# Gate vectors of a two-block transformer kernel: from one SBUF partition on ScalarE's queue to a DRAM copy on GpSimd's queue

## The chip, the cores and the metric

The kernel runs on one core of a Trainium2 chip. The metric is device time in microseconds, the median of several executions. All arithmetic is float32; large products are made of three passes, each on operands that were split into a high and a low part.

## The reference

A sequence of 256 tokens `x` (1024 features) and a context of 256 tokens `ctx` pass two blocks. The first has two layers. Each layer draws six vectors per stream from `c` (for the context from `c_ctx`): shift, scale and gate before and in each sublayer. The gates `g1`, `g2` are what this change touches.

```
m_lat = (silu(c) @ ada_w[i] + ada_b[i]);  m_ctx = silu(c_ctx) @ ada_w[i] + ada_b[i]
sh1, sc1, g1, sh2, sc2, g2 = split(m_lat, 6);  csh1, ..., cg2 = split(m_ctx, 6)
h, hc = rms(x) * (1 + sc1) + sh1, rms(y) * (1 + csc1) + csh1
o, oc = mixer(h, hc)              # layer 0: Fourier + window attention; layer 1: neighbourhood attention
x = x + g1 * o
x = x + g2 * swiglu(rms(x) * (1 + sc2) + sh2)
if not last: the same for the context y with cg1, cg2
```

The second block (retention, convolution, dilated attention, four swiglu) has no gates; it takes gains `norm_w_2` from DRAM.

## The kernel before

Tokens lie on partitions in two tiles of 128; each stream's activations transposed (`hT`, high and low part) are the stationary or moving side of the products. `Weights` (L205) streams the weights as blocks of 1 MB through three raw buffers on the SP queue: `load` (L242) issues the copy, `split` (L279) casts a block on ScalarE to its high part (`whi`) and subtracts on VectorE to its low part (`wlo`), by halves, into one of a few places. Every engine runs its instructions in the order of emission. That order is steered by `Pace` (L66), an account of when each engine would come to what has been emitted; it is an estimate of the program's own and moves nothing on the chip by itself. Its `note` (L127) charges a DMA issue with 1050 ns on GpSimd and 50 ns on another engine, and moves its one DMA clock `self.dma` on by the size of what is copied.

All instructions pass one helper (L60), so the profile's rows have that line; tile names tell them apart: `wraw` raw weight block, `acc` and `mm` PSUM, `hn` the normed tile, `ny` the inverse root on GpSimd, `jk` a sum of squares on ScalarE, `gate` a gate vector on all partitions, `rows` the six vectors as they come out.

The vectors are made in groups of 2048 outputs: group 0 is (sh1, sc1), group 1 (g1, sh2), group 2 (sc2, g2). `ada_unit` (L2093) multiplies one of eight blocks of inputs and adds the result into `rows`, a tile whose row 32 j (for x) and 32 j + 1 (for the context) hold outputs 512 j to 512 j + 511; at the first of the eight, the bias is loaded into it by GpSimd's queue. A gate vector thus lies in two single partitions, 512 numbers in each. `mods` (L2113) turns shift and scale into columns. `gate` (L2139) copies a gate to all 128 partitions, two DMAs on ScalarE's queue:

```
for h in range(2):
    r = 32 * (2 * x + h) + e
    nc.scalar.dma_start(out=t[:, h * 512:h * 512 + 512], in_=rows[r:r + 1, :]
                        .rearrange("p (a n) -> p a n", a=1).to_broadcast([1, 128, 512]))
```

The target is tile `gpost` (x) or `gpre` (context) of the pool `nb_p`, which hold one tile each and also serve layer 0's attention (its transposed probabilities `pt` and its mask), layer 1's `pt`, and the second block's gains (`gain`, L379, a GpSimd DMA from DRAM by `bcast_row`: one row of 1024 numbers for every partition). `gated` (L2150) multiplies the accumulator by the gate on VectorE and adds it to x.

`gate` is called at four places: in `Even.emit` before the output product (L1919, both streams), in the first feed-forward pair at its block 5 (L2182, both streams), in `Odd.emit` at its second quarter (L2073, x only) and in the second feed-forward at its block 5 (L2184, x only): six gates, twelve DMAs. In `Even.emit` the units of groups 1 and 2 are `fill`, work between the attention's steps: eight of group 1, then eight of group 2, so that sixteen additions to `rows` follow each other on VectorE. The output product of `Even` goes by `begin` and `tail` (two blocks for both token tiles, then the last two for tile 0 and for tile 1), first for x and then for the context. Layer 1's units are spread over the feed-forward pair (groups 0 and 1) and over `Odd` (group 2).

Of the kernel before, what the change touches and what calls it, by code (L numbers as in the profile page):

```python
# [7 lines left out]
F32 = mybir.dt.float32  # L8
# [4 lines left out]
PSUM = bass.MemoryType.PSUM  # L13

D = 1024
KD = 8
# [8 lines left out]
HOLD = 1200                # no split where a stage is due within this time ...  # L25
HOLD_AHEAD = 1             # ... unless fewer blocks than this are split ahead

# columns of the packed small inputs
# [9 lines left out]
# columns of the packed constants  # L38
# [11 lines left out]
class Engine:  # L50
    """Passes an engine's instructions on and keeps the pace's account of them."""
# [14 lines left out]
class Pace:  # L66
    """An estimate of when each engine comes to the instructions emitted so far, from the waits that
    the data needs and the price of each instruction. It only steers the order of emission."""

    LAG = {"pe": 190, "act": 40, "dve": 190, "pool": 190}       # from an engine's end to another's start  # L70
    OWN = {"pe": 0, "act": 190, "dve": 125, "pool": 125}        # ... to its own next instruction
# [12 lines left out]
    def entry(self, ap):  # L84
        """Times of the last write, of its engine, and of the last use, by element of the tile."""
        t = ap.tensor
        if t.name not in self.tiles:
            n = int(np.prod(t.shape[1:]))
            free = 0.0
            hist = self.tags.setdefault(t.tag, [])  # L90
            bufs = t.bufs or t.tag_meta.bufs
            if len(hist) >= bufs:
                free = max(x.max() for x in self.tiles[hist[-bufs]][:2])
            hist.append(t.name)
            self.tiles[t.name] = [np.full(n, free), np.full(n, free), ""]
        return self.tiles[t.name]
# [14 lines left out]
    def ready(self, *aps):  # L111
        """When the data of these is there for another engine."""
        return max(float(self.view(x, self.entry(x)[0]).max()) + self.LAG.get(self.entry(x)[2], 0) for x in aps)

    def free(self, tag, bufs, n):
        """When the next n tiles of this tag are free."""
# [3 lines left out]
    def loaded(self, tile):  # L120
        """A block of weights goes into this tile."""
# [45 lines left out]
    def clock(self, start, end):  # L167
        """The tensor engine runs at half its clock after a window in which it was mostly idle."""
# [36 lines left out]
class Weights:  # L205
    """Streams weight blocks: DRAM -> raw -> (high part, low part), ahead of their use.

    Blocks are split, by halves, where the pace has them landed and the engines that split them idle,
    so that no engine waits on a transfer with other work behind it."""

    def __init__(self, K):
# [4 lines left out]
        self.at = -1             # the last block asked for  # L216
        self.part = None         # the block of which one half is split
# [4 lines left out]
        self.slots = []          # free slots, the longest free first  # L222
# [11 lines left out]
    def close_slot(self, name):  # L234
        """No block goes into this slot any more."""
# [43 lines left out]
    def split(self, u):  # L279
        """The next half of block u."""  # L280
# [45 lines left out]
class Kernel:  # L326
# [3 lines left out]
    def open(self, ex):  # L330
# [13 lines left out]
        self.mm_n, self.held = 0, []         # tiles "mm" taken so far; those that put-off stages read: [number, task]  # L344
# [12 lines left out]
    def open_ext(self, n):  # L357
        """Room for one more weight block ahead; "3" is the place of the context's h^T."""
# [25 lines left out]
    def post(self, gain, bias=None):  # L384
        """x += rms(acc (+ bias)) * gain, in stages."""
# [31 lines left out]
    def block2(self, bin_):  # L417
        """bin_: the boundary before the first sublayer, its A of both tiles done."""
# [10 lines left out]
    def table(self, func):  # L429
        """Have the scalar engine fetch this function's table ahead of its use."""  # L430
# [13 lines left out]
    def rsqrt(self, ss, n, scale, eps, pool, tag="n", bufs=None):  # L444
        """1/sqrt(ss * scale + eps)."""
# [6 lines left out]
    def square(self, ss, src, b):  # L452
        """ss[:, b] = sum of the squares / D of src, half b of [tok, D]."""
# [4 lines left out]
    def rstd(self, ss):  # L458
        """1/sqrt(ss[:, 0] + ss[:, 1] + eps)."""
# [9 lines left out]
    def split_psum(self, hi, lo, ps, act=True):  # L469
        """hi + lo = ps exactly, each with the bits one fast pass carries."""  # L470
# [4 lines left out]
    def bcast_row(self, row, n):  # L475
        """DMA source: a DRAM row of n elements for every partition."""
        return bass.AP(row.tensor, row.offset, [[0, 128], [1, n]])

# [7 lines left out]
    def mm32(self, out, lhsT, rhs, start, stop, share=1, **k):  # L486
        """A float32 product; share: how many run side by side."""
# [7 lines left out]
    def mm_nat(self, key, hT, t, out, parity=False):  # L495
        """out[tok, 256] = h[tok tile t, or the tokens of parity t] @ w block (K = 1024)."""
# [7 lines left out]
    def mm_trans(self, key, hT, out, need=1):  # L504
        """out[feat, j, tok] = (h @ w block)^T for its two 128-feature tiles."""
# [26 lines left out]
    def room(self, tag, n):  # L532
        """Run put-off tasks of this tag until fewer than n are left."""
# [6 lines left out]
    def defer(self, f, src, need=1, tag=None):  # L540
        """Run f (which takes `need` PSUM tiles) once the tensor engine has come to where src is there."""
# [7 lines left out]
    def stage(self, f, src, eng, tag=None, after=None):  # L549
        """Emit f, work of the engine eng, once that engine need not wait for src and `after` holds."""  # L550
# [4 lines left out]
    def run(self, task):  # L555
        """Run a put-off task now, if it hasn't run."""
# [10 lines left out]
    def poll(self, need=3):  # L567
        """Run what is due, as long as it takes no more than `need` PSUM tiles."""
# [10 lines left out]
    def soon(self):  # L579
        """Whether a stage is about to be due."""  # L580
        return any(x[4] and x[0] <= self.t + HOLD and (x[5] is None or x[5]()) for x in self.tasks)

    def tick(self):
        """Run the stages that are due."""
# [17 lines left out]
    def acct(self, shape=(128, 512)):  # L602
        """Two banks."""
# [3 lines left out]
    def new_hT(self, e=0):  # L607
        """The place of x's (of the context's) h^T: high and low parts."""
# [6 lines left out]
    def transposed(self, h, halves=None):  # L615
        """The transposes of h[tok, 1024] in PSUM, by halves."""
# [5 lines left out]
    def transpose_h(self, halves, hT, t, cols=None):  # L622
        """Transposes of tile t into h^T's high and low parts; cols: (scale, shift) columns."""
# [19 lines left out]
    def transpose_into(self, src, chunk, t):  # L643
        """src[tok, 256] of tile t, transposed, into a chunk's high and low parts."""
# [12 lines left out]
    def begin(self, keys, chunks):  # L657
        """The first two blocks where the boundary before still holds the accumulators: tile 0 first."""
# [9 lines left out]
    def tail(self, keys, chunks, bound, start=0, accs=None, mid=None, late=False):  # L668
        """The last blocks of acc[t] = sum over blocks of chunk^T @ w: token tile 0 ends first."""
# [22 lines left out]
    def head(self, keys, fn, bound):  # L692
        """The first blocks of a product take token tile 0 before tile 1 is ready."""
# [17 lines left out]
class Bound:  # L711
    """What lies between two sublayers: the residual update and the next sublayer's h^T."""
# [9 lines left out]
    def load(self, which=(True, True)):  # L722
        """Fetch the gains, if any, of the norms after and before a sublayer of the second block."""
# [7 lines left out]
    def tile(self, t):  # L731
        """Where tile t's h comes to stand."""
# [6 lines left out]
    def A(self, t, acc=None):  # L739
        """The update by tile t's acc and the norm, in stages."""  # L740
# [16 lines left out]
        # tile 1 after tile 0's transposes  # L757
# [24 lines left out]
    def put_off(self, t):  # L782
        """Have the transposes done when tile t's h is there."""
# [18 lines left out]
class Ffn:  # L802
    """swiglu: (silu(h wg) * (h wu)) wd."""
# [11 lines left out]
    def order(self):  # L815
        """(kind, index) in the order of use."""
# [84 lines left out]
class FfnPair:  # L901
    """swiglu of x and of the context, on one pass over the weights of its first product: what the
    context's half of the second product takes waits on chip."""
# [23 lines left out]
    def emit(self, bins, bouts):  # L927
        K, nc, W = self.K, self.K.nc, self.K.W
        name, n, cut = self.name, self.NP, self.CUT
        with K.tc.tile_pool(name=f"{name}_sg", bufs=2, reuse_waits="tile") as sg_p, \  # L930
# [4 lines left out]
            def finish(p, js, q, e):  # L935
                """silu(g) * u of the feature tiles js: x's split, the context's kept."""
# [10 lines left out]
            def head(units):  # L947
                """Units (block, g or u, x or the context) whose operands come one after the other."""
# [71 lines left out]
class Retention:  # L1020
# [4 lines left out]
    def order():  # L1025
        """(kind, head, part) in the order of use; of the first head, what can take a token tile at a time comes first."""
# [17 lines left out]
    def emit(self, bin_, bout):  # L1044
# [6 lines left out]
        # decay by distance: exp(lgf * max(n - m, 0) + lgb * max(m - n, 0)), column n - m + 128 of row m  # L1051
# [122 lines left out]
class Conv:  # L1174
    PADL = 15
    W = 288                  # columns of a padded row of tokens
# [12 lines left out]
    def emit(self, bin_, bout):  # L1189
# [19 lines left out]
        def shift(p):  # L1209
            """Rows (j, i): channel i of each group of 32, from token j - 15 on."""  # L1210
# [32 lines left out]
        def glu(p, s, qa, qb):  # L1243
            """(qa + bias) * sigmoid(qb + bias), features on the partitions, tokens s."""
# [12 lines left out]
        def build():  # L1257
            """The products' weights for the next part of the convolution."""
# [9 lines left out]
        def conv(kt, c0, n, nat):  # L1268
            """Depthwise: four taps and 32 channels a product, four of them side by side."""
# [24 lines left out]
        def stats(t, b):  # L1294
            """Layernorm over channels in the natural layout, then back."""
# [55 lines left out]
        bout.hT = oT             # token tile by token tile, what comes next takes its place  # L1351
# [23 lines left out]
class Attn:  # L1375
    """Softmax attention of two heads by 128 queries a step; scores, transposes and values lie apart."""
# [16 lines left out]
    def require(self, pred=lambda step: True):  # L1393
        """Go on until no step for which pred holds is open."""
# [61 lines left out]
    def turn(self, step, sm):  # L1456
# [4 lines left out]
        w = 4 // n               # heads to a PSUM tile  # L1461
# [137 lines left out]
class Even:  # L1599
    """Layer 0's mixer: Fourier mixing and attention, for x and for the context."""  # L1600
# [769 lines left out]
```

## Time and profile before

| | |
|---|---|
| time, median of 3 runs | 2721.39 us (2714.77, 2721.39, 2721.40) |
| profiled execution, first to last instruction | 2716.9 us; nothing is listed around it |
| mean granted TensorE clock | 0.985 |
| TensorE busy | 2599.4 us (96%) |
| VectorE, ScalarE, GpSimd busy | 1496.4, 1202.4, 108.5 us |
| DMA | 453.68 MB, 167 GB/s over the span |

The profiled execution's own time is its span. The share of busy time is a mean over stages; what one stage waits for is read in the timeline, where `[4.78 <-ACT whi L60]` says that the engine sat idle for 4.78 us before this instruction and what it then waited for. A "q" behind an engine (ACTq, SPq) is that engine's sequencer, which issues DMAs.

### The profile page before, as it was taken

What the parts mean: (1) busy time and instruction counts of PE and PEld (TensorE: products, weight loads), DVE (VectorE), ACT (ScalarE), POOL (GpSimd) and SP (SyncE); (2) the same over time, 40 slices, a digit from 0 to 9 for tenths busy, and PEclk for the clock granted to TensorE, in tenths of its full rate; (3) what the DMA queues carried; (4) which work ended last, traced back from release to release, by engine and by line L of the source; (5) the groups of instructions that cost most, each with busy time, mean ns of one, the idle gap of its engine ahead of it and who ended that gap; (6) DMA issues with size and microseconds to landing.
All of it is one profiled execution on the core that took longest, in us unless ns stands there. A gap on an engine that the chain in (4) does not pass through costs nothing.

```text
span 2716.9 us, 43849 instructions
## 1 busy us (share of the span) xinstructions
PE 2599.4 (96%) x18444; PEld 2308.7 (85%) x18444; DVE 1496.4 (55%) x2420; ACT 1202.4 (44%) x2050; POOL 108.5 (4%) x156
## 2 busy tenths in 40 slices
PE   6988997999989999999999979999999999999998
PEld 5646875788867999999999869989998999999997
DVE  4475332346647745765645555456555654765643
ACT  4454221235535544544544434445554544544532
POOL 1100000000311000000000000000000000000000
PEclk9998998999989999999999999999999999999999
DMA  7368257545464675564655736545443654564652
GB/s 259 123 215 153 102 185 125 189 155 184 119 129 137 202 176 181 181 199 142 206 182 168 226 89 212 192 140 175 136 132 118 210 186 155 181 202 140 205 186 82
DMA packets 321414, 453.68 MB, mean 167 GB/s; under 512 B 20689, under 2 KB 280913, under 8 KB 316097
## 3 DMA queue, kind: packets, MB, share of 16 engines
q1 hardware_dynamic: 315552, 434.63, 48.1%
q10 hardware_dynamic: 2592, 5.33, 3.7%
q0 software_dynamic: 3072, 10.91, 1.1%
q8 instruction: 145, 2.38, 0.4%
q14 instruction: 53, 0.43, 0.0%
HBM read 445.47 MB, written 2.23 MB: 165 GB/s over the span
## 4 chain that ended last, share of the span: by engine, by line
PE 83%; DVE 6%; DMA 6%; ACT 2%; issue 1%; ACTq 0%; POOL 0%; SPq 0%; DVEq 0%; POOLq 0%
PE mm L60 62%; PE acc L60 21%; DVE wlo L60 2%; DMA wraw<-ev_w_out 1%; DMA wraw<-ada_w 1%; DMA wraw<-ffn_w_up 1%; DVE sm L60 1%; DVE hTl L60 1%; ACT whi L60 1%; DMA u<-up 1%; DMA wraw<-ffn_w_down 1%; ACTq L60 0%; DMA taps<-u 0%; POOL ny L60 0%; DVE hn L60 0%
## 5 line engine op out<-in xcount | busy, mean ns | idle before, releaser
L60 DVE TENSOR_TENSOR wlo<-wraw,whi 128x1024 fp32r<-128x1024 f32 x592 | 701.3, 1225 | 454.4 <-ACT whi L60 453.5
L60 ACT CAST whi<-wraw 128x1024 fp32r<-128x1024 f32 x592 | 592.4, 1048 | 392.7 <-issue 155.7
L60 PE MATMUL mm<-hTh,whi 128*128 128x256 f32 (+1 forms) x1840 | 553.5, 301 | 17.0 <-ACT whi L60 15.2
L60 PE MATMUL mm<-hTh,wlo 128*128 128x256 f32 (+1 forms) x1840 | 552.0, 300 | 0.6 <-DVE wlo L60 0.5
L60 PE MATMUL mm<-hTl,whi 128*128 128x256 f32 (+1 forms) x1840 | 551.9, 300 | 0.3 <-DVE hTl L60 0.3
L60 PE MATMUL mm<-whi,hTh 128*128 128x256 f32 x1616 | 467.8, 290 | 4.1 <-ACT hTh L60 3.2
L60 PE MATMUL mm<-whi,hTl 128*128 128x256 f32 x1616 | 458.7, 284 | 5.5 <-DVE hTl L60 5.5
L60 PE MATMUL mm<-wlo,hTh 128*128 128x256 f32 x1616 | 457.9, 283 | 0.0
L60 PEld LDWEIGHTS mm<-hTh,whi 128*128 128x128 f32 x1840 | 352.7, 192 | 32.0 <-ACT whi L60 16.0
L60 PEld LDWEIGHTS mm<-hTl,whi 128*128 128x128 f32 x1840 | 351.7, 191 | 13.5 <-DVE hTl L60 0.5
L60 PEld LDWEIGHTS mm<-hTh,wlo 128*128 128x128 f32 x1840 | 351.6, 191 | 13.0 <-DVE wlo L60 1.7
L60 PEld LDWEIGHTS mm<-whi,hTh 128*128 128x128 f32 x1616 | 310.4, 192 | 22.7 <-issue 9.7
L60 PEld LDWEIGHTS mm<-whi,hTl 128*128 128x128 f32 x1616 | 310.4, 192 | 7.6 <-DVE hTl L60 7.6
L60 PEld LDWEIGHTS mm<-wlo,hTh 128*128 128x128 f32 x1616 | 310.9, 192 | 0.6
L60 PE MATMUL acc<-whi,ckh 128*128 128x512 f32 x664 | 264.7, 399 | 0.0
L60 PE MATMUL acc<-whi,ckl 128*128 128x512 f32 x664 | 262.6, 395 | 0.6 <-DVE ckl L60 0.6
L60 PE MATMUL acc<-wlo,ckh 128*128 128x512 f32 x664 | 262.6, 395 | 0.4 <-DVE wlo L60 0.4
L60 PE MATMUL mm<-hTh 128*128 128x256 f32 x656 | 188.3, 287 | 0.5 <-ACT hTh L60 0.5
L60 PE MATMUL mm<-hTh,hTl 128*128 128x256 f32 x656 | 186.7, 285 | 0.4 <-DVE hTl L60 0.4
L60 PE MATMUL mm<-hTl,hTh 128*128 128x256 f32 x656 | 186.4, 284 | 0.0
L60 DVE TENSOR_TENSOR hTl<-wraw,hTh 128x1024 fp32r<-128x1024 f32 x116 | 138.9, 1223 | 59.0 <-ACT hTh L60 58.9
L60 DVE TENSOR_TENSOR sg<-sg,mm 128x512 f32<-128x512 f32 (+1 forms) x67 | 40.2, 600 | 228.2 <-PE mm L60 228.2
(245 smaller groups left out, 3335.2 us busy)
## 6 DMA issues: line engine op xcount, KB each, us to landing
wraw<-ffn_w_in SPq DMA_DIRECT2D x88, 1024.0 KB, 5.1
wraw<-ret_w_in SPq DMA_DIRECT2D x48, 1024.0 KB, 5.2
wraw<-ffn_w_out SPq DMA_DIRECT2D x44, 1024.0 KB, 4.9
wraw<-ada_w SPq DMA_DIRECT2D x40, 1024.0 KB, 5.2
wraw<-attn_w_in SPq DMA_DIRECT2D x36, 1024.0 KB, 5.0
wraw<-ffn_w_down SPq DMA_DIRECT2D x33, 1024.0 KB, 4.9
wraw<-ffn_w_gate SPq DMA_DIRECT2D x22, 1024.0 KB, 5.2
wraw<-ffn_w_up SPq DMA_DIRECT2D x22, 1024.0 KB, 5.3
```

The costliest lines, as they stand in the source:

```text
L60: r = f(*args, **kw)
```

## The change

The last `ada_unit` of groups 1 and 2 now also saves the four rows of each stream that needs them to a DRAM tile, one small DMA per stream on GpSimd's queue (two streams in layer 0, x alone in layer 1: six DMAs). `gate` reads the saved 1024 numbers from DRAM to all partitions with one DMA on GpSimd's queue, the same access that `gain` uses: six DMAs of 512 KB instead of twelve of 256 KB. The same places call it, and the tiles it writes are the same. Comments and docstrings go as well; those lines are left out here.

```diff
 ...
     def ada_unit(self, l, g, k, acc=None):
 ...
         nc.vector.tensor_tensor(out=t, in0=t, in1=ps, op=ALU.add)
+        if k == KD - 1 and g:
+            self.save_rows(l, g)
         self.W.done(("ada", l, g, k))
 ...
     def gate(self, l, n, e):
         nc = self.nc
         g, x = (1, 0) if n == "g1" else (2, 1)
-        rows = self.rows[l, g]
+        src = self.saved[l, g, e]
         t = self.nb_p.tile([128, D], F32, tag=("gpost", "gpre")[e], name="gate")
-        for h in range(2):
-            r = 32 * (2 * x + h) + e
-            nc.scalar.dma_start(out=t[:, h * 512:h * 512 + 512], in_=rows[r:r + 1, :].rearrange("p (a n) -> p a n", a=1).to_broadcast([1, 128, 512]))
+        nc.gpsimd.dma_start(out=t, in_=self.bcast_row(src[2 * x:2 * x + 2, :], D))
         self.gates[l, n, e] = t
 
+    def save_rows(self, l, g):
+        for e in range(1 if l else 2):
+            self.saved[l, g, e] = d = self.rows_p.tile([4, 512], F32, name=f"rows{l}{g}{e}")
+            self.nc.gpsimd.dma_start(out=d, in_=self.rows[l, g][e:e + 97:32, :])
+
 ...
-        K.rows, K.mod, K.gates = {}, {}, {}
+        K.rows, K.saved, K.mod, K.gates = {}, {}, {}, {}
+        K.rows_p = ex.enter_context(tc.tile_pool(name="saved", bufs=1, space=bass.MemoryType.DRAM))
```

## Rows read from the trace of the kernel before

**Rows 1.** Page, part 1: busy us (share of the span) x instructions.
```profile
PE 2599.4 (96%) x18444; PEld 2308.7 (85%) x18444; DVE 1496.4 (55%) x2420; ACT 1202.4 (44%) x2050; POOL 108.5 (4%) x156
```

**Rows 2.** Timeline of PE: start, us, instruction, idle time before it and its releaser.
```profile
197.50 0.66 PE L60 MATMUL mm<-pt,kv 128*64 128x128 f32 x8 [0.34 <-ACT pt L60]
...
198.94 0.47 PE L60 MATMUL acc<-whi,hTh 128*128 128x512 f32 x1
...
217.59 0.80 PE L60 MATMUL acc<-whi,hTh 128*128 128x512 f32 x1 [4.78 <-ACT whi L60]
...
247.33 1.94 PE L60 MATMUL mm<-consts,hn 128*128 128x128 f32 x8 [6.78 <-DVE hn L60]
...
452.54 0.80 PE L60 MATMUL mm<-hTh,whi 128*128 128x512 f32 x1 [13.35 <-ACT whi L60]
...
482.03 0.50 PE L60 MATMUL mm<-hTh,whi 128*128 128x512 f32 x1 [1.81 <-ACT whi L60]
...
786.33 1.94 PE L60 MATMUL mm<-consts,sm 128*128 128x128 f32 x8 [11.73 <-DVE sm L60]
```

**Rows 3.** Timeline of ACT and its queue, same columns.
```profile
203.95 12.45 ACTq L60 DMA_DIRECT2D gate<-rows  x1
216.50 3.88 ACT L60 CAST whi<-wraw 128x1024 fp32r<-128x1024 f32 x4 [16.56 <-issue]
...
242.14 1.99 ACT L60 CAST whi<-wraw 128x1024 fp32r<-128x1024 f32 x2 [10.24 <-DMA wraw<-ev_w_out]
...
451.44 1.99 ACT L60 CAST whi<-wraw 128x1024 fp32r<-128x1024 f32 x2 [22.49 <-DMA wraw<-ffn_w_up]
...
782.15 1.99 ACT L60 CAST whi<-wraw 128x1024 fp32r<-128x1024 f32 x2 [13.35 <-DMA wraw<-od_w_in]
```

**Rows 4.** Windows: stretch, length, busy PE PEld DVE ACT POOL, PEclk, DMA share, GB/s.
```profile
217.59:222.41 4.82, 4.35 (x9) 3.06 (x10) 4.82 (x5) 2.79 (x3) 0.00 (x0) 0.50 0.96 237
...
247.33:256.00 8.67, 8.67 (x31) 7.26 (x32) 7.76 (x12) 4.70 (x9) 0.00 (x0) 0.67 0.71 236
...
452.54:460.00 7.46, 7.43 (x21) 5.46 (x22) 2.34 (x2) 1.39 (x2) 0.00 (x0) 0.64 1.00 135
...
786.33:796.00 9.67, 9.67 (x58) 7.45 (x58) 8.71 (x32) 6.49 (x16) 2.22 (x2) 0.69 0.34 110
...
430.00:439.19 9.19, 9.19 (x41) 7.18 (x39) 1.68 (x3) 0.00 (x0) 0.00 (x0) 1.00 0.90 27
...
985.00:1000.00 15.00, 15.00 (x109) 14.10 (x108) 7.78 (x7) 7.08 (x8) 0.00 (x0) 1.00 0.91 51
```

**Rows 5.** DMA issues: count, KB each, median us from issue to landing.
```profile
gpre<-norm_w POOLq DMA_DIRECT2D x8, 512.0 KB, 5.7
...
gate<-rows ACTq DMA_DIRECT2D x12, 256.0 KB, 21.4
...
rows<-ada_rows POOLq DMA_DIRECT2D x5, 256.0 KB, 3.4
...
out<-x SPq DMA_DIRECT2D x2, 256.0 KB, 2.1
```

**Rows 6.** Timeline of SP's queue: start, us of issuing.
```profile
726.33 2.61 SPq L1966 DMA_DIRECT2D bias<-od_rel_bias  x4
...
755.19 16.30 SPq L1966 DMA_DIRECT2D bias<-od_rel_bias  x4
```

**Rows 7.** Tile gpre: its copies from DRAM, ns of issuing min/median/max.
```profile
L60 POOL DMA_DIRECT2D gpre<-norm_w x8: 527/528/952, 907.1 to 2324.7; - x8
```

**Rows 8.** Timeline of POOL, same columns as Rows 2.
```profile
226.03 0.57 POOL L60 TENSOR_TENSOR ny<-nv,half 128x1 f32<-128x1 f32 x1 [118.22 <-DVE nv L60]
...
277.77 1.49 POOL L60 DMA_DIRECT2D rows<-ada_rows  x2
```

**Rows 9.** Timeline of DVE: the eighth and ninth of sixteen additions to rows.
```profile
163.07 0.68 DVE L60 TENSOR_TENSOR rows<-rows,mm 128x512 f32<-128x512 f32 x1
...
170.66 0.68 DVE L60 TENSOR_TENSOR rows<-rows,mm 128x512 f32<-128x512 f32 x1
```

More of the change, by code (lines that the diff above doesn't have):

```diff
@@ L2159, in gated @@
         return update
-    for f in (ada_plan, ada_unit, mods, cols, gate, gated):
+    for f in (ada_plan, ada_unit, mods, cols, gate, save_rows, gated):
         setattr(Kernel, f.__name__, f)
```

## The prediction

> **What bounds the kernel now.** I read the page first, then the matrix engine's timeline between 100 and 1100 us, where alone the gates are loaded, then the queues of the engine it waited for. TensorE is busy 96% of the span [rows 1], so a change to copies can only pay where TensorE stands still. Its timeline has four long holes in that stretch [rows 2]: 4.78 us before 217.59, 6.78 before 247.33, 13.35 before 452.54 and 11.73 before 786.33; a fifth of 1.81 stands at 482.03. Elsewhere there it hardly stops, and beside the last gate call, at 985, not at all.
>
> Each long hole lies behind gate copies. At 203.95 ScalarE's queue spends 12.45 us issuing one gate copy; the next cast of a weight block (whi) starts at 216.50, after 16.56 us in which ScalarE waited for nothing but its own queue [rows 3]. TensorE needed that block at 212.81. The other three holes have another cause: the cast waits for the weight block itself. ScalarE idles 10.24 us for wraw<-ev_w_out until 242.14, 22.49 us for wraw<-ffn_w_up until 451.44 and 13.35 us for wraw<-od_w_in until 782.15 [rows 3]. In the second hole what TensorE names is VectorE's hn, because the squares that hn needs stand behind the late cast in ScalarE's order.
>
> Why the blocks are late is seen in the windows [rows 4]: from 430 to 439.19 the DMA engines are 90% busy and move 27 GB/s; at 985 to 1000 they are 91% busy at 51 GB/s. They are occupied by something that moves almost nothing. That is the gate copy: 256 KB each, median 21.4 us to land, twelve of them; 512 KB of gain from DRAM, on the GpSimd queue with the very same access (one row to every partition), takes 5.7 us [rows 5]. In Odd the SP queue shows the jam as well: four bias copies take 16.30 us to issue at 755.19 against 2.61 at 726.33, so the od_w_in block behind them goes out only at about 771.5 [rows 6].
>
> **What the change removes, hole by hole.** A hole costs its idle time and the slow matmuls that follow it: the granted clock is half or two thirds behind each [rows 4]. Loss by the clock is length times (1 - clock).
>
> First: 4.78 + 4.82 x 0.50 = 7.2 us. Second: 6.78 + 8.67 x 0.33 = 9.6. Third: 13.35 + 7.46 x 0.36 = 16.0, and the hole of 1.81 at 482.03, which comes while the weight stream is catching up and has no counterpart in the other turns of that loop: 17.8. Fourth: 11.73 + 9.67 x 0.31 = 14.7. Sum 49.4 us. The last gate (985) jams the DMA engines too, but TensorE has no hole [rows 4], so it gives 0.
>
> Would something else be late in their place? In the first stage TensorE does five turns of one block and one token tile from 198.94 to 212.81 [rows 2], 2.8 us each. The fourth block's place is free when the first block is done, after the third turn, about 207. From the start of a cast to the first matmul on it are 1.1 us (216.50 to 217.59) [rows 2, 3], so without the queue in the way the block is usable at 208 to 209, some 4 us before it is needed. The context's half of the same stage has the same order of work, no gate issue in front of it, and no hole behind the second one until the feed-forward begins near 282; that is my best evidence that nothing else binds. In the feed-forward loop the turns before 430 have no hole. In Odd, od_w_in would go out some 13.7 us earlier (16.30 - 2.61), more than the hole of 11.73.
>
> **What it adds.** Twelve GpSimd DMAs: six small saves (four rows of 2 KB to DRAM) and six gates of 512 KB. A GpSimd issue takes 0.53 to 0.95 us [rows 7], so 6.3 to 11.4 us of GpSimd time in total, on an engine busy 4% of the span [rows 1]. On its queue the first layer's gates stand after a gap of 118.22 us in which it has nothing to do until 226.03 [rows 8]. They wait there for TensorE's last read of pt at 197.50 + 0.66 [rows 2]; at a landing of 5.7 us the second is there by about 205, and VectorE multiplies by the first only when the tile's last block is through, after 212.81: some 8 us of cover. Layer 0's second gates need nothing newer than that stage, and GpSimd is free from 277.77 + 1.49 [rows 8]: they can go out there, 150 us before the stretch at 430 that the copies now jam. The two gates of layer 1 have their place free since the sublayer before. Nothing on GpSimd behind them waits for them to land.
>
> The saves make one new wait. GpSimd issues save (0,1) once VectorE's eighth row addition ends, and the load of group (0,2)'s rows stands behind it, where before nothing held it. The eighth addition ends at 163.07 + 0.68 = 163.75; the ninth, which needs the load, starts at 170.66 [rows 9]. Two issues are 1.1 to 1.9 us and the load lands in 3.4 [rows 5]: 168.3 to 169.1, so 1.6 to 2.4 us to spare. If this cover were gone (the two additions back to back) the cost would be 4.5 to 5.3 us of VectorE. The save has no row of its own; the nearest write to DRAM, the output's, lands in 2.1 us [rows 5], and the first gate that reads a save comes over 30 us after it (the closest pair, group (0,1)).
>
> New bytes for the DMA engines: the gates' total is unchanged (3 MB), now at the rate of the gains. Two gates hold up a weight block by at most the 5.7 us in which they land [rows 5]. Bounds for all that is new: 0 (hidden as above) to 5.3 + 5.7 = 11 us. I take 2.5, nearer to the hidden end, since every cover above holds by a row.
>
> The row says that the issue of a GpSimd copy takes 0.53 to 0.95 us while VectorE is 55% busy [rows 1, 7]. The Trainium skill, "SBUF — State Buffer", "Who interferes with whom", speaks against the move: descriptors of GpSimd's copies are written through a port that some VectorE operations lock, so a copy issued there can be held until such an operation ends, and it advises the scalar or sync queue for that reason. If by that rule each of the twelve waited out one VectorE operation as long as those of [rows 9], 0.68 us, that would be 8 us, were all exposed, and the sum would be 8 us worse; by the rows such holds are inside the 0.95.
>
> Also moved is the order of emission: Pace charges GpSimd 1050 ns for a DMA and ScalarE 50, and counts the saves in its account of the DMA, so splits of weight blocks may be emitted a little earlier or later from 163 us on. No row prices that. The rest of the kernel (1100 us to the end) uses the same code with no gate in it. I allow 8 us either way.
>
> **How the numbers follow.** The profiled execution's span is 2716.9; the three runs lie 2.1 below and 4.5 and 4.5 above it, on average 2.3 above, with the median 4.5 above. 2716.9 - 49.4 + 2.5 = 2670.0; plus 2.3, about 2672.
>
> **The rivals.**
> 1. Some of the holes come back, because there the weight stream had no slack or the changed order of emission puts a split later. One as dear as the third (16.0) gives 2688; the first two together (16.8) give 2689. For it: 1 MB of gates comes in the stage in which a block of 1 MB is used up every 5.5 us (two turns). Against: the second half of that stage. Chance 0.17.
> 2. The copy is slow because one row goes to all partitions, not because that row lies in one partition. Then only ScalarE's stall goes (7.2), and the third hole with the earlier issue (17.8): 2716.9 - 25.0 + 2.3 = 2694. The gain's 5.7 us for the same access speaks against it. Chance 0.03.
> 3. GpSimd's copies are held while VectorE works. Twelve holds of 0.68 us, all exposed, give 2672 + 8 = 2680; the 8 us of cover before the first gate's use say they would be hidden. Chance 0.03. (It is what the port rule of the Trainium skill's page, above, would do here.)
> 4. Nothing changes: the holes are those of weights that would be late anyway. Then 2719. Against it, 27 GB/s during the wait. Chance 0.02.
> 5. Slower: Pace, taking the GpSimd price and the saves into its DMA account, puts off splits in the feed-forward loop, so that ScalarE meets a block's cast only after TensorE wants it. The price of one such miss is the third hole's 16.0 us; the 49.4 gained are gone at the fourth miss (64), and the time is then about 2734. The loop has eleven turns, so there is room for four; the saves move Pace's DMA clock by no more than a microsecond or two each, which speaks against. Chance 0.04.
>
> My forecast, all four holes gone, has the rest: 0.71. Its own bounds are 2661 (8 us of luck in the order, nothing new exposed: 2672 - 2.5 - 8) and 2688 (all new costs, 8.5 us more than I took, and 8 us of bad order: 2672 + 16). The range reaches over rival 1 as well, with a few microseconds for its new costs: 2661 to 2692. A change of 0.3% is 8 us here, about what a measurement of this kernel can tell from none. Faster by more: forecast and rivals 1 to 3, 0.94; within it: rival 4, 0.02; slower: rival 5, 0.04.
>
> **What would show it.** Right: no DMA issue on ScalarE's queue beyond the first loads and the output; gate from rows saved, landing in 5 to 8 us; no hole above 2 us on TensorE at the four places, the clock full behind them; the four bias copies issued in about 2.6 us. Wrong: DMA engines 90% busy at under 60 GB/s beside a gate; VectorE waiting for the rows' load near 170 or for a gate; GpSimd's ny late behind a save in Odd; holes of the same size elsewhere in the feed-forward loop with the block landed and its cast emitted late.

## The result, and the profile after

| | before | after |
|---|---|---|
| time, median (lowest to highest), 4 runs each | 2721.39 us (2714.77 to 2722.09) | 2672.81 us (2669.99 to 2676.29) |
| profiled execution: span, its time | 2716.9, the same | 2668.3, 2670.09 |
| mean granted TensorE clock | 0.985 | 0.992 |

After to before 0.9832, 95% interval 0.9815 to 0.9849: 1.7% faster, where 2672 was predicted.

The page of the changed kernel (span; busy us, share and instructions of each engine; packets, MB and share of time of GpSimd's queue, q0, and ScalarE's, q10):

```profile
span 2668.3 us, 43859 instructions
PE 2590.2 (97%) x18444; PEld 2303.1 (86%) x18444; DVE 1496.5 (56%) x2420; ACT 1202.5 (45%) x2050; POOL 116.1 (4%) x168
...
q0 software_dynamic: 4128, 14.11, 1.5%
...
q10 hardware_dynamic: 864, 2.18, 0.2%
```

TensorE does the same 18444 matmuls in 9 us less of busy time than in [rows 1] (fewer of them at a low clock), and the rest of the 48.6 us that the span lost is idle time.

TensorE's timeline after: the first matmul of the output product, which answers to 198.94 in [rows 2], and every idle time above 1 us from there to 1000:

```profile
201.80 0.47 PE L60 MATMUL acc<-whi,hTh 128*128 128x512 f32 x1
...
268.25 0.38 PE L60 MATMUL mm<-hTh,whi 128*128 128x256 f32 x1 [1.81 <-ACT hTh L60]
...
741.16 1.06 PE L60 MATMUL mm<-consts,sm 128*128 128x128 f32 x8 [1.14 <-DVE sm L60]
...
749.44 0.41 PE L60 MATMUL mm<-consts,qn 128*128 128x128 f32 x2 [1.08 <-DVE qn L60]
...
819.44 1.09 PE L60 MATMUL mm<-kT,qT 64*128 64x512 f32 x2 [1.30 <-DVE sc L60]
...
855.26 0.39 PE L60 MATMUL mm<-whi,hTh 128*128 128x256 f32 x1 [1.80 <-ACT hTh L60]
```

None of the four long holes of [rows 2] is left, nor the fifth of 1.81 in the feed-forward loop; 268.25 and 855.26 are boundaries between sublayers. Three of the four casts of weight blocks that came late in [rows 3], in ScalarE's timeline of the changed kernel:

```profile
210.27 2.01 ACT L60 CAST whi<-wraw 128x1024 fp32r<-128x1024 f32 x2 [7.05 <-PE acc L60]
...
421.07 2.00 ACT L60 CAST whi<-wraw 128x1024 fp32r<-128x1024 f32 x2 [6.83 <-DMA wraw<-ffn_w_up]
...
736.98 2.00 ACT L60 CAST whi<-wraw 128x1024 fp32r<-128x1024 f32 x2 [2.75 <-DMA wraw<-od_w_in]
```

The first now waits for its place (TensorE's last read of an old block), not for ScalarE's queue. The one in the feed-forward loop waits 6.83 us for its block in place of 22.49; the casts of the three turns ahead of the hole waited as long in the kernel before (6.61 to 6.73 us) without a hole on TensorE. The one in Odd waits 2.75 us in place of 13.35. What the gates do instead, in GpSimd's timeline (two saves, the bias load behind them, the gates of the four calls):

```profile
166.90 1.19 POOL L60 DMA_DIRECT2D rows<-rows  x2 [57.39 <-DVE rows L60]
168.08 0.58 POOL L60 DMA_DIRECT2D rows<-ada_rows  x1
...
200.57 1.10 POOL L60 DMA_DIRECT2D gate<-rows  x2 [5.01 <-ACT hTh L60]
...
264.67 1.06 POOL L60 DMA_DIRECT2D gate<-rows  x2
...
704.48 0.60 POOL L60 DMA_DIRECT2D gate<-rows  x1
...
861.76 0.54 POOL L60 DMA_DIRECT2D gate<-rows  x1
```

And the stretches in which they land, by windows (columns as in [rows 4]):

```profile
200.00:212.00 12.00, 11.66 (x63) 9.71 (x62) 5.10 (x11) 4.36 (x7) 1.10 (x2) 1.00 0.90 344
264.00:276.00 12.00, 9.85 (x70) 9.42 (x69) 2.68 (x7) 2.64 (x6) 1.73 (x4) 0.86 0.41 132
704.00:716.00 12.00, 11.76 (x104) 11.22 (x104) 5.73 (x8) 2.63 (x7) 1.07 (x2) 1.00 0.66 219
861.00:873.00 12.00, 12.00 (x104) 12.00 (x103) 11.11 (x16) 9.67 (x16) 1.30 (x2) 1.00 0.85 263
```

The DMA engines are as busy behind the first gates as they were in the jams of [rows 4], 0.90, but move 344 GB/s instead of 27, and behind the later ones 132 to 263 with TensorE busy for most of each window: busy share alone did not show the jam, share and rate together did.

To say where the 48.6 us came from, both kernels are divided at six inverse roots (`ny` on GpSimd) that hold the same place in its work: in before they start at 104.51, 277.27, 605.50, 895.79, 1082.90 and 2711.62, in after at 106.75, 262.69, 570.84, 849.51, 1037.67 and 2663.33. Lengths between them, us, for these two and for the experiments' kernels (after_again is the changed kernel profiled once more):

| kernel | to the 1st | Even | pair | Odd | 2nd feed-forward | block 2 |
|---|---|---|---|---|---|---|
| before | 104.5 | 172.8 | 328.2 | 290.3 | 187.1 | 1628.7 |
| after | 106.8 | 155.9 | 308.2 | 278.7 | 188.2 | 1625.7 |
| after_again | 108.2 | 155.9 | 308.3 | 282.2 | 188.2 | 1626.5 |
| source_only | 106.4 | 155.2 | 308.3 | 281.2 | 188.2 | 1626.9 |
| queue_only | 106.6 | 176.5 | 331.0 | 293.7 | 201.0 | 1629.1 |
| own_partition | 106.3 | 154.5 | 308.1 | 281.1 | 188.2 | 1632.3 |
| order_kept | 104.8 | 155.1 | 308.3 | 279.5 | 188.0 | 1631.7 |
| only_even | 104.6 | 155.1 | 328.5 | 289.4 | 188.2 | 1628.1 |
| only_pair | 107.5 | 179.5 | 308.3 | 289.5 | 188.2 | 1628.6 |
| only_odd | 106.0 | 170.4 | 327.1 | 279.6 | 187.1 | 1628.0 |
| only_ffn1 | 106.4 | 172.1 | 327.3 | 289.4 | 188.1 | 1629.5 |
| bias_gpsimd | 105.9 | 155.0 | 308.3 | 302.9 | 192.8 | 1625.3 |
| bias_scalar | 105.0 | 154.8 | 308.3 | 313.4 | 191.4 | 1630.3 |

The first and last columns, where no gate is loaded, differ by some 3 us up or down between kernels that do the same there; differences of that size are not read there. The pair is steadier: 308.1 to 308.3 wherever its gates are changed, 327.1 to 328.5 in before and the three kernels that leave them, apart from queue_only. Odd is not: the changed kernel itself took 278.7 and 282.2 in its two profiles. After gains 16.9 us in Even, 20.1 in the pair and 11.6 in Odd (8.1 by after_again), and nothing in the second feed-forward.

The same three stages by windows, before and after (columns as in [rows 4]):

```profile
104.51:277.27 172.76, 147.32 (x884) 97.40 (x883) 110.42 (x273) 80.84 (x193) 4.97 (x7) 0.93 0.65 176
...
277.27:605.50 328.23, 309.93 (x1522) 248.29 (x1521) 115.43 (x158) 85.46 (x115) 1.99 (x3) 0.97 0.52 156
...
605.50:895.79 290.29, 273.63 (x1921) 227.94 (x1920) 187.49 (x427) 140.97 (x288) 49.50 (x41) 0.98 0.51 141
```

```profile
106.75:262.69 155.94, 141.21 (x884) 94.06 (x883) 110.22 (x273) 80.86 (x193) 8.42 (x14) 0.98 0.56 196
...
262.69:570.84 308.15, 306.00 (x1522) 246.73 (x1521) 115.45 (x158) 85.51 (x115) 3.62 (x6) 0.99 0.48 166
...
570.84:849.51 278.67, 272.21 (x1921) 226.64 (x1920) 187.73 (x427) 141.18 (x288) 51.54 (x43) 1.00 0.49 147
```

### The profile page after: what moved, and what is told of

Its sections match the earlier page's. It is cut to its first block, busy times and chain, and to the rows that moved or that the text cites. A ratio compares the mean times of both kernels' runs of the same rounds, so it can differ in the third digit from the quotient of the medians.

```text
span 2668.3 us, 43859 instructions
## 1 busy us (share of the span) xinstructions
PE 2590.2 (97%) x18444; PEld 2303.1 (86%) x18444; DVE 1496.5 (56%) x2420; ACT 1202.5 (45%) x2050; POOL 116.1 (4%) x168
## 4 chain that ended last, share of the span: by engine, by line
PE 85%; DVE 6%; DMA 3%; ACT 3%; issue 1%; POOL 1%; SPq 0%; POOLq 0%; DVEq 0%; ACTq 0%
PE mm L60 63%; PE acc L60 22%; DVE wlo L60 2%; DMA wraw<-ada_w 1%; DVE hTl L60 1%; DVE sm L60 1%; DVE hn L60 1%; POOL ny L60 1%; ACT whi L60 1%; ACT jk L60 1%; DMA wraw<-od_w_in 0%; ACT sm L60 0%; DMA u<-up 0%; DVE x L60 0%; ACT hTh L60 0%
## 5 line engine op out<-in xcount | busy, mean ns | idle before, releaser
L60 PEld LDWEIGHTS mm<-hTl,whi 128*128 128x128 f32 x1840 | 350.8, 191 | 13.3 <-DVE hTl L60 0.5
```

Of the source, the lines that this page charges most:

```text
L60: r = f(*args, **kw)
```

## The experiments

All shown edits are against the changed kernel; each median stands with its ratio to the kernel before, run on the same chip.

**Which part does it: the source or the queue?** Four kernels (queue_only, source_only, own_partition and order_kept) share one set of seven runs of before, median 2717.39 us. queue_only takes only the queue: the old copies from `rows`, issued by GpSimd, and no saves.

```diff
-        nc.gpsimd.dma_start(out=t, in_=self.bcast_row(src[2 * x:2 * x + 2, :], D))
+        for h in range(2):
+            r = 32 * (2 * x + h) + e
+            nc.gpsimd.dma_start(out=t[:, h * 512:h * 512 + 512], in_=self.rows[l, g][r:r + 1, :].rearrange(...).to_broadcast([1, 128, 512]))
```

> Gates still read from single SBUF partitions, two copies of 256 KB each, but issued by GpSimd; no saves to DRAM. Theory (the source in one partition makes the copy slow and jams the DMA engines): only ScalarE's queue stall goes (7 us); copies still take over 10 us to land at under 60 GB/s beside them, and holes in TensorE's timeline of 5 us or more remain, in the pair earlier than before since GpSimd's turn comes about 150 us earlier: 2690 to 2715 us. Rival (ScalarE's queue is what costs; the change of queue alone does it): no holes, 2676 us or less.

Measured 2743.4 us (2740.66 to 2745.92), ratio 1.0091 (1.0076 to 1.0106): slower than before, and above the time expected. TensorE's long idle times in it:

```profile
227.20 1.16 PE L60 MATMUL mm<-consts,hn 128*128 128x128 f32 x8 [4.07 <-DVE hn L60]
...
243.27 0.79 PE L60 MATMUL acc<-whi,hTh 128*128 128x512 f32 x1 [10.64 <-ACT whi L60]
...
327.44 0.37 PE L60 MATMUL mm<-hTh,wlo 128*128 128x256 f32 x1 [11.70 <-issue]
...
341.40 0.80 PE L60 MATMUL mm<-hTh,whi 128*128 128x512 f32 x1 [5.28 <-ACT sg L60]
...
776.63 0.58 PE L60 MATMUL mm<-whi,hTh 128*128 128x256 f32 x1 [10.24 <-ACT v L60]
...
947.97 0.69 PE L60 MATMUL mm<-consts,sgh 128*128 128x128 f32 x2 [10.94 <-DVE sgh L60]
```

The jam of the third hole did not go with an earlier issue, it moved. GpSimd issued the second call's four copies at 285.06, and the windows of the stretch behind that, the cast that then waited, and the tile's copies (ns of issuing, min/median/max; landing) say the rest:

```profile
288.65:315.70 27.05, 26.71 (x206) 26.46 (x207) 4.38 (x6) 2.96 (x4) 0.00 (x0) 0.94 0.95 27
```

```profile
330.01 2.00 ACT L60 CAST whi<-wraw 128x1024 fp32r<-128x1024 f32 x2 [30.82 <-DMA wraw<-ffn_w_gate]
```

```profile
L60 POOL DMA_DIRECT2D gate<-rows x12: 536/536/599, 199.9 to 920.5; - x12
...
DMA to landing us min/median/max: 11.9/21.2/40.1
```

Median landing 21.2 us against 21.4 in [rows 5]: the queue changes nothing in the copy. The second call's four copies are 1.05 MB; at the window's 27 GB/s that is 39 us, and the longest of them took 39.1 (the 40.1 is of the first call).

Most of the holes stand behind casts that waited for a late block, as in before: 16.81 us for ev_w_out until 242.17, 16.27 for od_w_in until 774.32, 15.03 for ffn_w_up until 944.14. The 4.07 before 227.20 comes of the gate itself, for which VectorE's multiplication waited 3.5 us. The longest, 11.70 before 327.44, is another thing: it lies in the middle of one block's matmuls, ends 2.6 us before the late cast starts, and the profile names nothing that TensorE waited for (`issue`). Between 100 and 1100 us no matmul of any other kernel here has such a wait of over 0.3 us. What the trace does show is that the DMA queue of kind `instruction` (q8) brings packets 9, 24 and 45 us after the loop's first matmul in before (282.84), and 9, 25 and 46 us after it in the changed kernel (268.25), but in queue_only none from 279 to 325, and one at 325 to 326, when the jam has ended. That TensorE had run out of instructions, whose copies were jammed like the weights, is inferred from this and not tested; a gap alone does not make such a wait, since one from 411 to 467, around the third hole of before, made none.

The fourth call was free in before because it came at 985; issued at 920, it opens a hole of 10.94, and the second feed-forward takes 13.9 us more. Nor did it help to free ScalarE's queue alone: its stall of 12.45 us [rows 3] went, and Even is still 3.7 us longer.

source_only takes only the source: the saves, and the DRAM copy issued where the old ones were.

```diff
-        nc.gpsimd.dma_start(out=t, in_=self.bcast_row(src[2 * x:2 * x + 2, :], D))
+        nc.scalar.dma_start(out=t, in_=self.bcast_row(src[2 * x:2 * x + 2, :], D))
```

> Gates read from the DRAM copy, but issued by ScalarE's queue at its old place. Theory (the source): copies land in 4 to 8 us, no issue above 1 us on ScalarE's queue, no hole: 2667 to 2678 us. Rival (ScalarE's queue): an issue there still holds ScalarE for several us and the first hole of 7 us stays, 2680 us or more.

Measured 2672.14 us (2669.72 to 2675.31), 0.983 (0.9815 to 0.9845): the whole gain. Tile gate in it:

```profile
L60 ACTq DMA_DIRECT2D gate<-rows x6: 326/348/445, 200.1 to 941.4; - x6
...
DMA to landing us min/median/max: 3.5/4.4/7.4
```

No issue is longer than 0.45 us. The 12.45 us of [rows 3] belonged to the slow copies, then, not to ScalarE's queue as such.

**One partition, or SBUF as the source?** own_partition keeps SBUF, ScalarE's queue and the two halves, and lets each partition read its own row; there are no saves. It leaves the broadcast out, so the values are not the gates; bytes, targets and times of issue are.

```diff
-        nc.gpsimd.dma_start(out=t, in_=self.bcast_row(src[2 * x:2 * x + 2, :], D))
+        for h in range(2):
+            nc.scalar.dma_start(out=t[:, h * 512:h * 512 + 512], in_=self.rows[l, g])
```

> As the kernel before, two copies of 256 KB per gate on ScalarE's queue and SBUF as the source, but every partition's part comes from its own partition of the rows tile, so the values of the gates are not the gates: the broadcast is left out. Theory (one source partition is the bottleneck): 256 KB land in 3 to 6 us, the holes go, 2667 to 2680 us. Rival (SBUF as source, the halves, or ScalarE's queue are slow in themselves): over 10 us to land, 2690 us or more.

Measured 2676.31 us (2673.97 to 2677.66), 0.9842 (0.9825 to 0.9858). Tile gate:

```profile
L60 ACTq DMA_DIRECT2D gate<-rows x12: 472/616/818, 199.3 to 940.9; - x12
...
DMA to landing us min/median/max: 2.3/2.5/8.7
```

The same 256 KB take a median of 2.5 us from 128 partitions and 21.4 from one. (The 21.4 include waiting for the other copies of the same call: in before the shortest took 12.0 us, the longest of four 35.6.) So what was slow is the reading of one partition 128 times over, neither SBUF nor the queue. The Trainium skill, "SBUF — State Buffer", "Door 1: The DMA port swizzle", says that a transfer's rate depends on how many ports its partitions reach, and gives 27.6 GB/s, measured, for partitions that share one. The windows' 27 GB/s, in [rows 4] and here, agree. Whether the limit is the partition's own or that of a port which it shares with others, no run here separates.

**Did the order of emission add or take anything?** order_kept issues after's copies past Pace and notes the old ones in their stead; the instructions of TensorE, VectorE and ScalarE then stand in the order of before.

```diff
-        nc.gpsimd.dma_start(out=t, in_=self.bcast_row(src[2 * x:2 * x + 2, :], D))
+        nc.gpsimd.eng.dma_start(out=t, in_=self.bcast_row(src[2 * x:2 * x + 2, :], D))
+        for h in range(2):
+            r = 32 * (2 * x + h) + e
+            nc.note("act", "dma_start", (), dict(out=t[:, h * 512:h * 512 + 512], in_=self.rows[l, g][r:r + 1, :].rearrange(...).to_broadcast([1, 128, 512])))
...
-            self.nc.gpsimd.dma_start(out=d, in_=self.rows[l, g][e:e + 97:32, :])
+            self.nc.gpsimd.eng.dma_start(out=d, in_=self.rows[l, g][e:e + 97:32, :])
```

> The changed kernel's copies, but the pace is told of the old ones, so that TensorE, VectorE and ScalarE have exactly the old order of instructions. Theory (the order of emission adds nothing): within 4 us of the changed kernel, 2668 to 2677 us. Rival (part of the gain, or of the loss against the sum, comes from the changed order): 2680 us or more, or 2664 us or less.

Measured 2673.82 us (2673.19 to 2674.48), 0.9836 (0.9821 to 0.985) against 0.9832: the order is worth nothing that shows.

**Does each hole give what its term says?** Four kernels make the change at one of the four calls alone; for Even:

```diff
-        if k == KD - 1 and g:
+        if k == KD - 1 and (l, g) == (0, 1):
             self.save_rows(l, g)
...
+        if (l, n) == (0, "g1"):
+            src = self.saved[l, g, e]
+            nc.gpsimd.dma_start(out=t, in_=self.bcast_row(src[2 * x:2 * x + 2, :], D))
+        else:
             ... # the loop of before, on nc.scalar
```

> Only layer 0's first gates (both streams) come by way of DRAM on GpSimd's queue; the other three calls are as before. Theory (the holes add up as in the sum): the first two holes go, 17 us, so 2721 - 17 = 2704 us (ratio 0.994). Rival (holes are passed on: time won here is waited for at the next hole): no more than 5 us, 2716 us.

> Only layer 0's second gates (both streams) are changed. Theory: the third hole and its after-effects go, 18 to 20 us, 2701 to 2703 us (ratio 0.993). Rival (passed on): 2716 us.

> Only layer 1's first gate is changed. Theory: 11.6 us by the two traces, 14.7 by the sum of the prediction: 2707 to 2710 us (ratio 0.995). Rival (passed on): 2717 us or more.

> Only layer 1's second gate is changed, the one whose slow copies had no hole beside them. Theory: no change, 2719 to 2723 us (ratio 0.999 to 1.001). Rival (slow copies cost something everywhere, by contention that the timeline does not show as a wait): 2715 us or less.

| kernel | measured us | ratio (95%) |
|---|---|---|
| only_even | 2703.36 (2700.70 to 2703.61) | 0.9934 (0.9919 to 0.9949) |
| only_pair | 2707.43 (2705.94 to 2709.14) | 0.9950 (0.9934 to 0.9967) |
| only_odd | 2708.32 (2705.34 to 2710.31) | 0.9953 (0.9939 to 0.9968) |
| only_ffn1 | 2719.98 (2718.66 to 2724.41) | 1.0001 (0.9991 to 1.0010) |

The product of the four is 0.984, against 0.9832 for all at once. By stages they add up as well: Even 17.7 us shorter in only_even, the pair 19.9 in only_pair, Odd 10.7 in only_odd, 48.3 together, against 16.9, 20.1 and 11.6, together 48.6, in the changed kernel. only_pair missed what was expected of it by some 5 us. Its pair stage is 19.9 us shorter, as it should be, but Even, which it leaves as before, is 6.7 longer. ScalarE's timeline there:

```profile
201.46 18.26 ACTq L60 DMA_DIRECT2D gate<-rows  x4
219.75 5.78 ACT L60 CAST whi<-wraw 128x1024 fp32r<-128x1024 f32 x6 [18.12 <-issue]
```

All four gate issues of Even run on, and six half casts stand behind them, where in before four did [rows 3]: the saves in Pace's account had moved one block's split behind the issues. TensorE's two holes there grew to 7.58 and 8.70 us. So the order seems to cost, beside slow copies, which is argued from this one kernel; order_kept shows that it costs nothing once they are gone.

**Can more be had?** In after the late od_w_in block of Odd still stands on the SP queue behind four of the 32 bias copies. To see whether that is what delays it, two kernels give all 32 to another queue, `nc.gpsimd` or `nc.scalar` for `nc.sync` in line 1966, beside the changed kernel once more.

> The changed kernel once more, on the chip of the two kernels below: 2668 to 2677 us, ratio to the kernel before 0.981 to 0.985.

> The changed kernel with layer 1's bias copies (32 of 96 KB in short pieces) on GpSimd's queue instead of SP's, so that weight blocks no longer stand behind them. Theory (what is left of the fourth hole comes from od_w_in standing behind those copies): the 3.3 us of holes between 741 and 751 go, and Odd gets 3 us shorter (279 to 276), in all about 0.1%. Rival (the short pieces slow the DMA engines from any queue, or GpSimd's own work waits behind their issue): Odd as long as before or longer, same or slower.

> The same copies on ScalarE's queue. Theory: od_w_in goes out 3 us earlier as well, but 2.7 us of issuing per group of four now hold ScalarE, whose casts TensorE waits for: Odd between 276 and 282 us, total within 0.15% of the changed kernel. Rival (a queue stall as in the first hole, over 5 us): Odd 285 us or more.

Measured after_again 2675.37 us (0.9862, 0.9821 to 0.9903; one execution of six took 2710.64, at a mean granted clock of 0.924 where the others had 0.990 or 0.991, and it alone puts the ratio above the expected 0.985: the medians' ratio is 0.9841), bias_gpsimd 2697.64 (0.9927, 0.9911 to 0.9942), bias_scalar 2710.01 (0.9961, 0.9948 to 0.9973): both slower than the changed kernel, against the theory of both, nearly all of it in Odd and a little behind it. On ScalarE's queue the issues themselves are long:

```profile
649.99 12.16 ACTq L60 DMA_DIRECT2D bias<-od_rel_bias  x8
```

On GpSimd's they stand ahead of the inverse roots and of the gate, which itself now waits:

```profile
655.40 5.27 POOL L60 DMA_DIRECT2D bias<-od_rel_bias  x8
660.84 1.02 POOL L60 TENSOR_TENSOR ny<-nv,half 128x4 f32<-128x4 f32 x1 [0.16 <-DVE nv L60]
...
713.74 0.58 POOL L60 DMA_DIRECT2D gate<-rows  x1 [1.04 <-DMA bias<-od_rel_bias]
719.01 1.80 POOL L60 TENSOR_TENSOR bias<-bias,mask 128x768 f32<-128x768 f32 x1 [4.69 <-DMA bias<-od_rel_bias]
```

Pace prices these issues too, so the order moved with them; which of the two did the damage was not separated, and so neither kernel settles what the bias copies on SP's queue cost in after. No version beat the changed kernel.

## Why the prediction was right

**The cause.** The step that the copy is slow because its row lies in one partition, argued from the gain's 5.7 us [rows 5], holds: the gates land in 5.7 us now, and source_only and own_partition remove the holes by the source alone.

```profile
gpre<-norm_w POOLq DMA_DIRECT2D x8, 512.0 KB, 5.3
...
gate<-rows POOLq DMA_DIRECT2D x6, 512.0 KB, 5.7
...
rows<-rows POOLq DMA_DIRECT2D x6, 8.0 KB, 5.3
```

(DMA issues of the changed kernel, columns as in [rows 5].)

**The terms.** First and second hole 16.8 predicted, Even gained 16.9. Third, with the 1.81 behind it, 17.8; the pair gained 20.1: the term was 2 us short. By the windows above TensorE's idle time in the pair fell by 16.2 us (15.2 in the term) and its busy time, for the same 1522 matmuls, by 3.9 (2.7 in the term), so both parts of the term were a little small. The last gate 0, as only_ffn1 shows. Fourth 14.7; Odd gained 11.6, and 8.1 in after_again, 9.1 in source_only, 9.2 in own_partition. By the windows its idle time fell by 10.2 us (11.7 in the term) and its busy time, for the same 1921 matmuls, by 1.4 (3.0 in the term). Its block was to go out 13.7 us earlier. SP's queue after:

```profile
720.83 2.73 SPq L1966 DMA_DIRECT2D bias<-od_rel_bias  x4
723.66 0.89 SPq L253 DMA_DIRECT2D wraw<-od_w_in  x1
```

The four bias copies take 2.73 us, against 16.30 in [rows 6]. After runs 34.7 us ahead by then (570.84 against 605.50), so the block's issue at 723.66 answers to 758.3 in before's time, 13.3 us before its 771.6. But it lands 13.3 us later, at 736.98, where in before it took 10.6 (771.6 to 782.15). So it comes 10.5 us earlier, less than the hole of 11.73; the cast still waits 2.75, and TensorE has short stops from 741 to 751 (1.14 and 1.08 us are the longest). That a block issued in time also lands in time was the part of this term that failed; it can account for the idle time that is left, some 1.5 us of the 3. The other half, slow matmuls, and the 3.5 us by which after_again gained less again are not traced. Why the block lands late is open: from 723.66 to 736.98 the DMA engines are 75% busy at 204 GB/s, with the bias copies and an ada_w block under way beside it.

**The new costs.** 2.5 us taken; no wait that would be one is seen. The new wait behind the save, in VectorE's timeline, the eighth and ninth additions of [rows 9]:

```profile
165.93 0.68 DVE L60 TENSOR_TENSOR rows<-rows,mm 128x512 f32<-128x512 f32 x1
...
173.51 0.68 DVE L60 TENSOR_TENSOR rows<-rows,mm 128x512 f32<-128x512 f32 x1
```

They start 7.58 us apart, 7.59 before: the load came in time. The save lands in 5.3 us, not the 2.1 taken from the output's write, a wrong size without effect, as the first gate is issued 33.7 us behind it. The second gates did go out early, at 264.67. Of the 8 us allowed for the order, order_kept shows about 1, less than its interval can tell from none.

**The sum.** Span 2670.0 predicted, 2668.3 measured; the errors of the terms (0.1, 2.3, -3.1), 1.1 lost in the second feed-forward, the 2.5 not paid and 1 us net in the stages without gates make up the difference. That it came so close is in part luck: the errors of the third and the fourth term cancel, and the changed kernel's own runs lie 6 us apart.

**The rivals.** 1, that a hole returns: no. 2, that only the queue's part goes: no, and its own price (2694) was wrong. It let the third hole go with the earlier issue; queue_only shows that an early slow copy jams the weights just as long, and gains nothing. 3, GpSimd held by VectorE: a gate's issue takes 0.533 to 0.597 us on GpSimd, less than the 0.68 of one addition, and source_only, off GpSimd's queue, takes the same time. The hold that the Trainium skill describes in "SBUF — State Buffer", "Who interferes with whom", does not show in these issues or in the kernel's time; the landing is 1.3 us longer on GpSimd's queue (5.7 against 4.4), whether by such a hold or not, and nothing waited for it. 4, that nothing changes, and 5, that the kernel gets slower: no.

## What to carry to other kernels

A DMA that reads one SBUF partition for all 128 went at 27 GB/s here, far below what the DMA engines move from many partitions or from DRAM, and it holds the DMA engines for everyone: look for a window with a high DMA share and a low rate, and for the weight cast that then waits. A short trip through DRAM cures it, and in this kernel it did not matter which queue issued the copy. Issuing a slow copy earlier is no cure; ask whether the stretch it moves into has work ahead for as long as it takes.

## What was not expected of the hardware

A change of queue alone cost 0.9%: the copies were as slow as before, and the fourth call, free at 985, opened a hole of 10.94 us when it was issued at 920. In the same kernel TensorE stood 11.70 us in the middle of a block's matmuls without any wait that the profile names, and went on about 2 us after the first packet of the instruction queue behind the jam. A save of 8 KB takes 5.3 us to land on GpSimd's queue, as long as a 512 KB gain. ScalarE's queue spent 12.45 us on one gate issue behind three slow ones, and a median of 0.35 us in source_only.
